# A two-block transformer in fp32 halves: MLP products with hi and lo side by side, and moving weights of 512 columns

## The chip, the cores and the metric

The kernel runs on one core of a Trainium2 chip. The metric is the device time of one execution in microseconds. The kernel before took 950.4 us (median of three runs, 950.13 to 951.17).

## The reference, cut to what matters

The input is one sequence of 256 tokens with 1024 features. It passes two blocks of two layers each: in the first block MoBA with forgetting attention, then differential with sliding-window attention; in the second block MLA, a cross-attention to a memory of 256 tokens and an MLP, then a stick-breaking attention, again a cross-attention and an MLP. The change touches the cross-attention's memory side and the MLP:

```python
def mem_cross_attn(h, m, w_q, w_kv, w_o):
    q = (h @ w_q).reshape(B, S, MEM_HEADS, MEM_HEAD_DIM)
    kv = (m @ w_kv).reshape(B, m.shape[1], 2, MEM_HEADS, MEM_HEAD_DIM)   # 1024 -> 512 keys, 512 values
    ...
def sq_relu_mlp(h, w_in, w_out):                                          # 1024 -> 4096 -> 1024
    return jnp.square(jax.nn.relu(h @ w_in)) @ w_out
```

All arrays are float32.

## The kernel before, in words

Each projection is made of three matmuls in fp32r. A weight and an activation are each split into a rounded part (hi) and the rest (lo); the product is hi x hi + hi x lo + lo x hi, summed in PSUM. Weights come from HBM by SyncE's queue in pieces of 512 KB ([128, 1024]); `wpiece` and `split` (lines 635 to 656) cut each in two parts of 512 columns, copy the hi part (ScalarE or VectorE) and subtract for the lo part (VectorE). Activations are kept by features (`x` as four tiles [128, 2, 256]), and `new_T` (line 715) makes the split tiles: for chunks of 128 features hi and lo tiles that each hold two chunks.

There are two kinds of projection. `mm_feat` has 128 weight columns stationary and 256 tokens moving, so the result stands by features. `mm_tok` has 128 tokens stationary and up to 512 weight columns moving, so the result stands by tokens.

`mlp` (line 1533) runs G = 8 groups of 512 hidden features. `hidden(g)` makes a group: `proj_feat` with four blocks of 128 features, two to a PSUM bank of 512 columns; per block ReLU out of PSUM, a square, and a split. Its product with `wout` goes on into four accumulator banks that live through the whole MLP; the group after is started before it. The first MLP (`final=False`) does this product with `mm_feat` and adds each bank to `x` by `add_x`, times a broadcast scale (`rstd_bc`). The second (`final=True`) does it with `mm_tok`.

`mem_kv(l)` makes a memory's keys and values for one cross-attention. It is written ahead of the stage that needs it and depends on nothing in it, so its parts fill gaps. The values are made in two passes of 256 columns, both token tiles side by side in one bank; each half is drained when its pass is done.

The order of the work is not written by hand: `Plan.schedule` (line 303) simulates the engines with a table of costs and starts, on each engine, the ready operation with the longest way to the end. It reckons N/2.4 + 2 ns for an fp32r matmul of N columns, a transfer at 360 bytes per ns plus `LANDING`, and it adds to each priority a random number of spread `SHAKE` (0 before). A buffer of a pool (8 PSUM banks; classes acc, S, T, O, F have upper limits) is given ahead of its turn only while enough stay for what comes before it in the program. All instructions are issued from one helper, so nearly every record carries line 569; matmuls are told apart by shape. Tiles carry their pool's name: `k` is float32, `r` is fp32r, `psum` a bank.

Of the kernel before, what the change touches and what calls it, by code (L numbers as in the profile page):

```python
# [14 lines left out]
AF = mybir.ActivationFunctionType  # L15
OP = mybir.AluOpType
# [137 lines left out]

AHEAD = 4000.0

LANDING = 2500.0

FIRST = {"T": 1200.0, "A": 700.0, "V": 1200.0, "G": 800.0, "S": 730.0}

SHAKE, SEED = 0.0, 0

LAT = {("T", "A"): 196, ("T", "V"): 196, ("T", "G"): 196, ("A", "T"): 271, ("V", "T"): 256, ("G", "T"): 203,
       ("A", "A"): 143, ("V", "V"): 127, ("G", "G"): 102, ("A", "V"): 142, ("V", "A"): 128, ("A", "G"): 170,
# [9 lines left out]
class Plan:  # L174
# [95 lines left out]
    def schedule(self):  # L270
# [58 lines left out]
        while n < len(ops):  # L329
# [72 lines left out]
            if o.kind == "dma_start":  # L402
# [3 lines left out]
                free[e] = t + issue  # L406
                o.start, o.end = t, st + d + LANDING
            else:
# [165 lines left out]
S = 256  # L574
D = 1024
NT = 2
NC8 = D // 128
FF = 4096
# [52 lines left out]
class Net:  # L631
# [82 lines left out]

    def new_T(self, n=NC8):

        res = []
        for nm in ("xh", "xl"):
            v = []
            for c0 in range(0, n, 2):  # L720
                t = self.r2([128, min(2, n - c0), 256], nm)
                v += [t[:, c] for c in range(min(2, n - c0))]
            res.append(v)
        return res

    def mm3(self, ps, st, mv, first, last):

# [731 lines left out]
    def mem_kv(self, l):  # L1459

        w = self.a["xa_w_kv_2"][l]
        mt = self.gained(self.memT, 48 + 8 * l)
        kT = self.new_T(4)
        for b in range(4):
            ps = self.ps("F")[:, :256]
            for wh, wl, k, n in self.wtiles(w, 0, NC8, b * 128, 128, "f"):
                for i in range(n):
                    self.mm_feat(ps, k + i == 0, mt, wh[:, i], wl[:, i], k + i, k + i == NC8 - 1)
            y = self.t2([128, 256], "xy")
            self.nc.vector.tensor_tensor(y, ps, self.rmem_bc, op=OP.mult)  # L1470
            self.split(y, kT[0][b], kT[1][b])
        v = [[self.r2([128, 512], "xv") for _ in range(NT)] for _ in range(2)]
        for b in range(2):
            ps = self.ps("F")
            for wh, wl, k, n in self.wtiles(w, 0, NC8, 512 + b * 256, 256, "f"):
                for t in range(NT):
                    s = slice(t * 128, (t + 1) * 128)
                    for i in range(n):
                        h, lo = mt[0][k + i][:, s], mt[1][k + i][:, s]
                        o = ps[:, t * 256:(t + 1) * 256]  # L1480
                        f = dict(stop=False, skip_group_check=True)
                        self.nc.tensor.matmul(o, h, wh[:, i], start=k + i == 0 and t == 0, **f)
                        self.nc.tensor.matmul(o, h, wl[:, i], start=False, **f)
                        f["stop"] = k + i == NC8 - 1
                        self.nc.tensor.matmul(o, lo, wh[:, i], start=False, **f)
            for t in range(NT):
                o = slice(b * 256, (b + 1) * 256)
                self.evac_split(v[0][t][:, o], v[1][t][:, o], ps[:, t * 256:(t + 1) * 256], self.rmem[:, t:t + 1])
        self.xk[l], self.xv[l] = kT, v

    def cross(self, l):
# [41 lines left out]
    def mlp(self, l, final=False):  # L1533
        nc, a, xt = self.nc, self.a, self.xt
        win, wout = a["mlp_w_in_2"][l], a["mlp_w_out_2"][l]
        G = FF // 512
        if final:
            nc.boost = 2e4
            xf = self.x_tok()
            nc.seen = nc.ops[-1]  # L1540
            nc.boost = 0.0
        else:
            rb2 = self.rstd_bc(self.rstd2)
        acc = [self.acc() for _ in range(4)]

        def hidden(g):
            ps = self.proj_feat(win, xt, g * 512, 512, cls=("S", "T") if g % 2 else ("S", "O"))
            h = self.new_T(4)
            for b, p in enumerate(ps):
                for i in range(2):  # L1550
                    sq = self.t2([128, 256], "msq")
                    pi = p[:, i * 256:(i + 1) * 256]
                    r = self.t2([128, 256], "mr")
                    nc.scalar.activation(r, pi, AF.Relu)
                    nc.either(("V", "tensor_tensor", (sq, r, r), {"op": OP.mult}),
                              ("A", "activation", (sq, r, AF.Square), {}))
                    self.evac_split(h[0][2 * b + i], h[1][2 * b + i], sq)
            return h

        h = hidden(0)  # L1560
        for g in range(G):
            hn = hidden(g + 1) if g + 1 < G else None
            if final:
                pieces = [(hf, p) for hf in range(2) for p in self.wtiles(wout, 4 * g, 4, hf * 512, 512)]
                pieces = [(t, *p) for p in pieces for t in range(NT)]
                if g == G - 1:

                    rest = self.ps("S")
                    end = [(wh[:, :, c:c + 256], wl[:, :, c:c + 256], k, n, c) for c in (0, 256)
                           for t, hf, (wh, wl, k, n) in pieces if (t, hf) == (1, 1)]  # L1570
                    pieces = [p for p in pieces if p[:2] != (1, 1)]
                for t, hf, (wh, wl, k, n) in pieces:
                    nc.boost = 0.0 if g < G - 1 else 6e3 - 1.5e3 * (2 * hf + t)
                    self.mm_tok(acc[2 * hf + t], h, wh, wl, n, k - 4 * g, t, k == 0, k + n == FF // 128)
                nc.boost = 0.0
                if g == G - 1:
                    for wh, wl, k, n, c in end:
                        nc.boost = 1.0e3 if c == 0 else 0.0
                        self.mm_tok((rest if c else acc[3])[:, 0:256], h, wh, wl, n, k - 4 * g, 1, c > 0 and k == 4 * g,
                                    k + n == FF // 128)  # L1580
                    nc.boost = 0.0
                h = hn
                continue
            for hf in range(2):
                for wh, wl, k, n in self.wtiles(wout, 4 * g, 4, hf * 512, 512):
                    for b in range(4):
                        bank = 2 * hf + b // 2
                        o = acc[bank][:, (b % 2) * 256:(b % 2) * 256 + 256]
                        s = slice(b * 128, (b + 1) * 128)
                        for j in range(n):  # L1590
                            self.mm_feat(o, k + j == 0 and b % 2 == 0, h, wh[:, j, s], wl[:, j, s], k + j - 4 * g,
                                         k + j == 4 * G - 1)
                        if k + n == 4 * G and b % 2:
                            self.add_x(acc[bank], bank, rb2)
            h = hn
        if final:
            self.finish(xf, acc, rest)
# [187 lines left out]
```

## Time and profile before

| | |
|---|---|
| runs, median (lowest to highest) | 950.4 us (950.13 to 951.17) |
| the profiled execution, its own time | 950.25 us |
| its span, first to last instruction | 948.5 us |
| mean granted TensorE clock | 0.999 of full |
| HBM read | 154.89 MB |

Times below are microseconds from the start of the span unless marked ns. A stretch is a window of the span. "Busy" is the time in which an engine had at least one instruction running; matmul records overlap, since the engine is pipelined, so the mean ns of a matmul's record is longer than the distance to the next one.

### The profile page before, as it was taken

How to read it: one execution, taken by the hardware profiler on the slowest of the kernel's cores; microseconds unless marked ns; L12 is line 12 of the kernel's file. 1: busy time of each engine (PE TensorE's matmuls, PEld its weight loads, DVE VectorE, ACT ScalarE, POOL GpSimd, SP SyncE). 2: the span in 40 equal slices, each digit the busy share in tenths (PEclk: the TensorE clock that was granted, in tenths of full speed). 3: DMA queues.
4: the chain of work that ended last, by engine and by line, in shares of the span. 5: the costliest groups of instructions: out<-in, count | busy, mean ns of one | idle time of the engine just before them, and what ended most of it. 6: DMA issues, size and time to landing. Idle time of an engine off the chain costs nothing.

```text
span 948.5 us, 18213 instructions
## 1 busy us (share of the span) xinstructions
PE 934.5 (99%) x6852; PEld 874.0 (92%) x6852; DVE 675.1 (71%) x1568; ACT 579.7 (61%) x1317; POOL 57.1 (6%) x96
## 2 busy tenths in 40 slices
PE   8999999999999999999999999999999999999997
PEld 7898898889899999999999999999899999999986
DVE  9799978778978658974555556846859876666564
ACT  7687965687576856755554556536856745333353
POOL 1160000311401000000000000000000000000000
PEclk9999999999999999999999999999999999999999
DMA  8755346445325526554554667445526455555641
GB/s 312 233 177 178 111 142 219 158 128 157 122 79 167 167 68 202 176 156 124 171 193 160 221 217 233 134 151 179 178 67 203 135 174 178 182 193 192 199 147 44
DMA packets 45512, 157.12 MB, mean 166 GB/s; under 512 B 5352, under 2 KB 5488, under 8 KB 45424
## 3 DMA queue, kind: packets, MB, share of 16 engines
q1 hardware_dynamic: 44784, 154.59, 50.6%
q8 instruction: 53, 0.87, 0.4%
q0 software_dynamic: 352, 1.06, 0.3%
q10 hardware_dynamic: 288, 0.32, 0.1%
q14 instruction: 35, 0.29, 0.1%
HBM read 154.89 MB, written 1.06 MB: 164 GB/s over the span
## 4 chain that ended last, share of the span: by engine, by line
PE 92%; DVE 4%; DMA 1%; ACT 1%; issue 1%; POOL 0%; POOLq 0%; ACTq 0%; DVEq 0%; SPq 0%
PE psum L569 92%; DVE k L569 2%; DVE r L569 2%; DMA k<-in_w_in_ab_dram 1%; ACT r L569 1%; DMA k<-in_consts_dram 1%; ACT k L569 0%; POOL k L569 0%; POOLq L1779 0%; ACTq L569 0%; DVEq L569 0%; SPq L569 0%; POOLq L569 0%
## 5 line engine op out<-in xcount | busy, mean ns | idle before, releaser
L569 PE MATMUL psum<-r,r 128*128 128x256 f32 (+1 forms) x6078 | 884.3, 303 | 3.0 <-ACT r L569 2.0
L569 PEld LDWEIGHTS psum<-r,r 128*128 128x128 f32 x6078 | 802.9, 190 | 49.1 <-issue 5.7
L569 DVE TENSOR_TENSOR r<-k,r 128x512 fp32r<-128x512 f32 (+4 forms) x681 | 413.3, 644 | 159.9 <-PE psum L569 109.3
L569 ACT ACTIVATE r<-k 128x512 fp32r<-128x512 f32 (+2 forms) x587 | 321.1, 591 | 182.0 <-PE psum L569 150.4
L569 ACT ACTIVATE k<-psum 128x256 f32<-128x256 f32 (+4 forms) x163 | 68.0, 446 | 122.0 <-PE psum L569 119.7
L569 PE MATMUL psum<-k,k 128*128 128x128 f32 (+7 forms) x746 | 130.8, 304 | 3.0 <-DVE k L569 2.3
L569 PEld LDWEIGHTS psum<-k,k 128*128 128x128 f32 (+2 forms) x746 | 89.5, 166 | 16.4 <-DVE k L569 5.0
L569 POOL TENSOR_TENSOR k<-k,k 128x2 f32<-128x2 f32 (+3 forms) x42 | 48.1, 1162 | 860.7 <-DVE k L569 808.4
L569 ACT ACTIVATE k<-k 128x256 f32<-128x256 f32 (+5 forms) x154 | 73.0, 501 | 14.0 <-DVE k L569 10.7
L569 ACT ACTIVATE k<-k,k 128x256 f32<-128x256 f32 (+3 forms) x139 | 59.5, 447 | 8.8 <-DVE k L569 6.7
L569 DVE CAST r<-k 128x512 fp32r<-128x512 f32 (+3 forms) x94 | 36.4, 393 | 15.3 <-PE psum L569 7.4
L569 DVE TENSOR_TENSOR k<-k,k 128x512 f32<-128x512 f32 (+5 forms) x93 | 44.7, 491 | 1.6 <-ACT k L569 1.1
L569 DVE TENSOR_TENSOR k<-psum,k 128x512 f32<-128x512 f32 (+2 forms) x61 | 36.7, 607 | 11.6 <-PE psum L569 11.0
L569 ACT ACTIVATE r<-k,k 128x256 fp32r<-128x256 f32 x76 | 35.0, 500 | 12.1 <-DVE k L569 11.2
L569 DVE SCALAR_TENSOR_TENSOR r<-k,k,r 128x256 fp32r<-128x256 f32 x80 | 36.4, 478 | 0.7 <-PE psum L569 0.6
L569 DVE TENSOR_TENSOR k<-k 128x256 f32<-128x256 f32 (+3 forms) x34 | 11.8, 346 | 27.3 <-ACT k L569 25.8
L569 DVE TENSOR_TENSOR r<-psum,r 128x256 fp32r<-128x256 f32 (+1 forms) x36 | 18.0, 508 | 15.5 <-ACT r L569 14.3
L569 ACT ACTIVATE r<-psum 128x256 fp32r<-128x256 f32 (+1 forms) x36 | 16.2, 455 | 19.7 <-PE psum L569 19.6
L569 DVE TENSOR_SCALAR k<-k,k 128x8 f32<-128x8 f32 (+6 forms) x100 | 25.1, 282 | 1.5 <-POOL k L569 0.9
L569 DVE SCALAR_TENSOR_TENSOR k<-psum,k 128x256 f32<-128x256 f32 (+2 forms) x24 | 12.2, 508 | 5.6 <-PE psum L569 4.9
L469 ACT ACT_TABLE_LOAD x12 | 15.4, 1283 | 0.2
L569 DVE CUSTOM_DVE_ANT_0 k<-psum,k 128x256 f32<-128x256 f32 (+1 forms) x48 | 15.0, 350 | 0.6 <-PE psum L569 0.6
(39 smaller groups left out, 160.2 us busy)
## 6 DMA issues: line engine op xcount, KB each, us to landing
k<-in_mlp_w_in_dram SPq DMA_DIRECT2D x64, 512.0 KB, 4.3
k<-in_mlp_w_out_dram SPq DMA_DIRECT2D x64, 512.0 KB, 4.2
k<-in_w_in_ab_dram SPq DMA_DIRECT2D x29, 512.0 KB, 5.4
k<-in_w_in_cd_dram SPq DMA_DIRECT2D x26, 512.0 KB, 4.1
k<-in_sb_w_qkv_dram SPq DMA_DIRECT2D x24, 512.0 KB, 4.2
k<-in_xa_w_kv_dram SPq DMA_DIRECT2D x16, 512.0 KB, 4.2
k<-in_w_out_ab_dram SPq DMA_DIRECT2D x8, 512.0 KB, 3.9
k<-in_w_out_cd_dram SPq DMA_DIRECT2D x8, 512.0 KB, 3.8
```

The costliest lines, as they stand in the source:

```text
L469: self.nc.scalar.preload_act_table_set(table)
L569: return getattr(eng, method)(*[real(a) for a in args], **{k: real(v) for k, v in kw.items()})
```

## The change

- `new_T` makes one tile [128, 512] for each chunk, hi in columns 0 to 255, lo in 256 to 511, in place of separate hi and lo tiles of two chunks.
- `hidden(g)` goes over a group in two pairs of blocks. Each block has a PSUM bank of its own. Per chunk, wh meets the whole tile (512 columns: hi and lo) and wl meets the hi half (256 columns, into the first half of the bank). The two halves are then added: a copy of the second half, an add, and one instruction for max(r, 0) x r. The weight pieces are 4 chunks x 256 columns, before 2 chunks x 512.
- The first MLP's second product uses `mm_tok`; at its end each of the four accumulators is scaled by tokens, turned by 16 transposes and added to `x`. The broadcast scale is dropped there.
- `mem_kv` makes the values by `proj_tok` with 512 columns, in two banks of class F at once.
- The planner's `LANDING` goes from 2500 to 3500 ns, `SHAKE` from 0 to 150 ns with seed 9.

```diff
-LANDING = 2500.0
+LANDING = 3500.0
...
-SHAKE, SEED = 0.0, 0
+SHAKE, SEED = 150.0, 9
...
     def new_T(self, n=NC8):
-        res = []
-        for nm in ("xh", "xl"):
-            v = []
-            for c0 in range(0, n, 2):
-                t = self.r2([128, min(2, n - c0), 256], nm)
-                v += [t[:, c] for c in range(min(2, n - c0))]
-            res.append(v)
-        return res
+        t = [self.r2([128, 512], "xt") for _ in range(n)]
+        return [u[:, 0:256] for u in t], [u[:, 256:512] for u in t], t
...
         v = [[self.r2([128, 512], "xv") for _ in range(NT)] for _ in range(2)]
-        for b in range(2):
-            ps = self.ps("F")
-            for wh, wl, k, n in self.wtiles(w, 0, NC8, 512 + b * 256, 256, "f"):
-                for t in range(NT):
-                    s = slice(t * 128, (t + 1) * 128)
-                    for i in range(n):
-                        h, lo = mt[0][k + i][:, s], mt[1][k + i][:, s]
-                        o = ps[:, t * 256:(t + 1) * 256]
-                        f = dict(stop=False, skip_group_check=True)
-                        self.nc.tensor.matmul(o, h, wh[:, i], start=k + i == 0 and t == 0, **f)
-                        self.nc.tensor.matmul(o, h, wl[:, i], start=False, **f)
-                        f["stop"] = k + i == NC8 - 1
-                        self.nc.tensor.matmul(o, lo, wh[:, i], start=False, **f)
-            for t in range(NT):
-                o = slice(b * 256, (b + 1) * 256)
-                self.evac_split(v[0][t][:, o], v[1][t][:, o], ps[:, t * 256:(t + 1) * 256], self.rmem[:, t:t + 1])
+        for t, ps in enumerate(self.proj_tok(w, mt, 512, 512, cls="F", fill="f")):
+            self.evac_split(v[0][t], v[1][t], ps, self.rmem[:, t:t + 1])
...
-        else:
-            rb2 = self.rstd_bc(self.rstd2)
...
         def hidden(g):
-            ps = self.proj_feat(win, xt, g * 512, 512, cls=("S", "T") if g % 2 else ("S", "O"))
             h = self.new_T(4)
-            for b, p in enumerate(ps):
-                for i in range(2):
+            for b2 in range(2):
+                ps = [self.ps("S", "hid"), self.ps("T" if b2 else "O", "hid")]
+                for wh, wl, k, n in self.wtiles(win, 0, NC8, g * 512 + b2 * 256, 256):
+                    for b, p in enumerate(ps):
+                        s = slice(b * 128, (b + 1) * 128)
+                        for i in range(n):
+                            f = dict(skip_group_check=True)
+                            nc.tensor.matmul(p, wh[:, i, s], xt[2][k + i], start=k + i == 0, stop=False, **f)
+                            nc.tensor.matmul(p[:, 0:256], wl[:, i, s], xt[0][k + i], start=False,
+                                             stop=k + i == NC8 - 1, **f)
+                for b, p in enumerate(ps):
+                    r = self.t2([128, 256], "mr")
+                    half = self.t2([128, 256], "mh")
+                    nc.scalar.activation(half, p[:, 256:512], AF.Copy)
+                    nc.vector.tensor_tensor(r, p[:, 0:256], half, op=OP.add)
                     sq = self.t2([128, 256], "msq")
-                    pi = p[:, i * 256:(i + 1) * 256]
-                    r = self.t2([128, 256], "mr")
-                    nc.scalar.activation(r, pi, AF.Relu)
-                    nc.either(("V", "tensor_tensor", (sq, r, r), {"op": OP.mult}),
-                              ("A", "activation", (sq, r, AF.Square), {}))
-                    self.evac_split(h[0][2 * b + i], h[1][2 * b + i], sq)
+                    nc.vector.scalar_tensor_tensor(sq, r, 0.0, r, op0=OP.max, op1=OP.mult)
+                    self.evac_split(h[0][2 * b2 + b], h[1][2 * b2 + b], sq)
             return h
...
                 for wh, wl, k, n in self.wtiles(wout, 4 * g, 4, hf * 512, 512):
-                    for b in range(4):
-                        bank = 2 * hf + b // 2
-                        o = acc[bank][:, (b % 2) * 256:(b % 2) * 256 + 256]
-                        s = slice(b * 128, (b + 1) * 128)
-                        for j in range(n):
-                            self.mm_feat(o, k + j == 0 and b % 2 == 0, h, wh[:, j, s], wl[:, j, s], k + j - 4 * g,
-                                         k + j == 4 * G - 1)
-                        if k + n == 4 * G and b % 2:
-                            self.add_x(acc[bank], bank, rb2)
+                    for t in range(NT):
+                        self.mm_tok(acc[2 * hf + t], h, wh, wl, n, k - 4 * g, t, k == 0, k + n == FF // 128)
+                if g == G - 1:
+                    y = []
+                    for t in range(NT):
+                        y.append(self.t2([128, 512], "my"))
+                        self.scaled(y[t], acc[2 * hf + t], self.rstd2[:, t:t + 1])
+                    for b in range(2):
+                        p = self.ps("T")
+                        for c in range(2):
+                            for t in range(NT):
+                                o = (2 * b + c) * 128
+                                self.tr(p[:, (2 * c + t) * 128:(2 * c + t + 1) * 128], y[t][:, o:o + 128])
+                        self.add_x(p, 2 * hf + b)
```

## Rows read from the trace of the kernel before

**Rows 1.** The page: busy us, share and instructions of each engine; granted clock in 40 slices.
```profile
PE 934.5 (99%) x6852; PEld 874.0 (92%) x6852; DVE 675.1 (71%) x1568; ACT 579.7 (61%) x1317; POOL 57.1 (6%) x96
...
PEclk9999999999999999999999999999999999999999
```
**Rows 2.** The page: the chain that ended last, share of the span by engine.
```profile
PE 92%; DVE 4%; DMA 1%; ACT 1%; issue 1%; POOL 0%; POOLq 0%; ACTq 0%; DVEq 0%; SPq 0%
```
**Rows 3.** Groups by form, TensorE: tiles, shapes, count | busy us, mean ns | idle before.
```profile
L569 PE MATMUL psum<-r,r 128*128 128x256 f32 x5064 | 704.7, 286 | 1.5 <-DVE r L569 0.7 <-ACT r L569 0.7
L569 PE MATMUL psum<-r,r 128*128 128x512 f32 x918 | 264.3, 396 | 1.5 <-ACT r L569 1.3 <-DVE r L569 0.2
```
**Rows 4.** Timeline of TensorE, 455.8 to 475: start, us of the whole row, form, count.
```profile
455.78 19.42 PE L569 MATMUL psum<-r,r 128*128 128x256 f32 x160
```
**Rows 5.** Timeline of TensorE, 929 to 937.
```profile
928.80 8.55 PE L569 MATMUL psum<-r,r 128*128 128x512 f32 x37
```
**Rows 6.** Timeline of TensorE, 800 to 900: both forms, named by the first.
```profile
799.75 100.50 PE L569 MATMUL psum<-r,r 128*128 128x256 f32 x643
```
**Rows 7.** Groups by form, TensorE, of the same stretch, 800 to 900.
```profile
L569 PE MATMUL psum<-r,r 128*128 128x256 f32 x428 | 77.2, 280 | 0.0
L569 PE MATMUL psum<-r,r 128*128 128x512 f32 x215 | 74.5, 394 | 0.0
```
**Rows 8.** Table by stretch, 430 to 575: length, busy us and count of each engine, clock, DMA.
```profile
430.00:575.00 145.00, 145.00 (x1215) 145.00 (x1215) 80.55 (x148) 76.58 (x165) 0.70 (x1) 1.00 0.59 188
```
**Rows 9.** Groups by form over the whole span, VectorE and ScalarE.
```profile
L569 DVE TENSOR_TENSOR r<-k,r 128x512 fp32r<-128x512 f32 x561 | 367.5, 688 | 119.1 <-PE psum L569 87.1 <-ACT r L569 17.0 <-issue 12.7
L569 ACT ACTIVATE r<-k 128x512 fp32r<-128x512 f32 x490 | 286.1, 624 | 164.0 <-PE psum L569 145.7 <-DMA k<-in_w_in_ab_dram 5.4 <-DVE r L569 3.7
...
L569 DVE TENSOR_TENSOR r<-k,r 128x256 fp32r<-128x256 f32 x96 | 39.2, 426 | 36.5 <-PE psum L569 20.8 <-ACT r L569 15.3
...
L569 DVE SCALAR_TENSOR_TENSOR r<-k,k,r 128x256 fp32r<-128x256 f32 x80 | 36.4, 478 | 0.7 <-PE psum L569 0.6
L569 ACT ACTIVATE r<-k,k 128x256 fp32r<-128x256 f32 x76 | 35.0, 500 | 12.1 <-DVE k L569 11.2 <-PE psum L569 0.7
...
L569 DVE CAST r<-k 128x512 fp32r<-128x512 f32 x71 | 29.8, 424 | 6.1 <-PE psum L569 5.4 <-DMA k<-in_w_in_ab_dram 0.7
...
L569 ACT ACTIVATE k<-psum 128x256 f32<-128x256 f32 x75 | 25.4, 378 | 96.7 <-PE psum L569 95.8 <-DVE r L569 0.9
...
L569 DVE TENSOR_TENSOR k<-psum,k 128x256 f32<-128x256 f32 x16 | 6.7, 420 | 3.8 <-PE psum L569 3.4 <-ACT k L569 0.2
...
L569 DVE SCALAR_TENSOR_TENSOR k<-k,k,k 128x256 f32<-128x256 f32 x12 | 5.6, 476 | 0.3 <-ACT k L569 0.3
...
L569 DVE SCALAR_TENSOR_TENSOR k<-psum,k,k 128x512 f32<-128x512 f32 x4 | 3.0, 751 | 5.3 <-PE psum L569 5.3
```
**Rows 10.** Timeline at the end of both cross-attentions, TensorE: in brackets idle before and releaser.
```profile
397.36 0.39 PE L569 MATMUL psum<-r,r 128*128 128x256 f32 x1 [0.73 <-DVE r L569]
...
745.18 0.39 PE L569 MATMUL psum<-r,r 128*128 128x256 f32 x1 [0.39 <-ACT r L569]
```
**Rows 11.** Timeline of TensorE from 393.66: transposes (128 columns, k,k) among fp32r products.
```profile
393.66 0.27 PE L569 MATMUL psum<-k,k 128*128 128x128 f32 x1
393.69 0.37 PE L569 MATMUL psum<-r,r 128*128 128x256 f32 x1
393.90 0.27 PE L569 MATMUL psum<-k,k 128*128 128x128 f32 x1
393.92 0.37 PE L569 MATMUL psum<-r,r 128*128 128x256 f32 x1
```
**Rows 12.** Timeline at the end of the first MLP, 596 to 616: VectorE's adds and TensorE.
```profile
595.60 1.29 DVE L569 TENSOR_TENSOR k<-psum,k 128x512 f32<-128x512 f32 x2 [1.27 <-PE psum L569]
595.76 12.63 PE L569 MATMUL psum<-r,r 128*128 128x256 f32 x104
```
**Rows 13.** The page: DMA issues, count, KB each, median us from issue to landing.
```profile
k<-in_mlp_w_in_dram SPq DMA_DIRECT2D x64, 512.0 KB, 4.3
```

## The prediction

> **What bounds the kernel now.** I read the page's engine shares first, then its chain, then the groups by form, then stretches of TensorE's own timeline. TensorE is busy 99% of the 948.5 us span and the granted clock is at its upper level (2.4 GHz) in all forty slices [rows 1]; the chain that ended last runs 92% through matmuls into PSUM [rows 2]. Busy share alone proves little, because matmul records overlap: a 128x256 product has a record of 286 ns but takes up far less of the engine. What decides is the distance from one matmul to the next, and the groups say which forms there are: 5064 of 256 moving columns, 918 of 512, and before both together 3.0 us of idle [rows 3].
>
> The distance is read from stretches with nothing but one form. From 455.78 us, 160 products of 256 columns take 19.42 us: less the last record's 0.28, over 159 steps, 120.4 ns each [rows 4]. From 928.80 us, 37 products of 512 take 8.55 us: (8.55 - 0.39)/36 = 226.7 ns each [rows 5]. So 256 more columns cost 106.3 ns, and 14.1 ns of each matmul do not depend on its columns. This is the number on which the forecast stands. The test is a mixed stretch: from 799.75 to 900.25 us the second MLP runs 643 products [rows 6], 428 of 256 and 215 of 512 [rows 7]; 427 x 120.4 + 215 x 226.7 = 100.15 us, against 100.50 - 0.39 = 100.11 us measured. The two prices hold when the forms alternate, and these 100 us hold no wait at all. In the first MLP (430 to 575 us) TensorE and its weight loads are both busy throughout, VectorE 56%, ScalarE 53% [rows 8]. The kernel there goes as fast as matmuls can be issued; only fewer or narrower matmuls help.
>
> **Part 1, first products of both MLPs.** Now each of 8 groups x 4 blocks x 8 chunks needs three products of 256 (wh with x's hi, wh with x's lo, wl with x's hi). After, hi and lo lie side by side, and wh meets both in one product of 512; wl's stays. The columns are the same, the matmuls two in place of three: 256 removed a layer, 512 in all, each worth 14.1 ns [rows 4, 5]: 7.2 us off the bounding engine.
>
> What it adds: a block's halves must be summed. Before: ReLU out of PSUM, a square, the split. After: copy of the lo half (ScalarE, 378 ns), an add that reads PSUM (VectorE, 420), a combined max-and-multiply (476), the split (its lo 426) [rows 9]. VectorE's load for one MLP group is then 16 weight splits x 688 + 4 x (420 + 476 + 426) = 16.3 us, against 32 x (226.7 + 120.4) + 48 x 226.7 = 22.0 us of TensorE: 74%. I cost it at nothing; TensorE's own products hide it. That cover would be gone if VectorE also took all hi copies of the weights (16 x 424 ns [rows 9] make 23.1 us, 1.1 a group and 9 an MLP too many), but those are ScalarE's first, whose 16 x 624 + 4 x 378 = 11.5 us leave room.
>
> PSUM: a pair of blocks now fills two banks in 5.6 us where four blocks filled two in 11.6. With four accumulators there are two pairs, so one is drained (2 x 1.3 us of VectorE by the rows above) while the other fills: nothing, as long as memory's products don't hold banks (first rival).
>
> The entry into each MLP changes. The first pass over all eight chunks now takes 5.6 us, not 11.6, while chunks are still being made at 500 ns (ScalarE) and 478 (VectorE) each [rows 9]. The second pair's products on early chunks can cover it. Nothing in the trace shows this order. Below it costs nothing (a gain is out: the only waits of TensorE near the entries are those priced in Part 3), above 2 us an entry (four late chunks at 500 ns); I take 0.5 each, the size of the waits seen there [rows 10]: 1.0 us.
>
> **Part 2, second product of the first MLP.** 768 products of 256 become 384 of 512, now with the hidden values as weights: 384 x 14.1 = 5.4 us. The result then stands by tokens and must be turned: four scalings and 16 transposes. Where transposes and 256-column products alternate, a pair takes 0.23 to 0.24 us [rows 11], so a transpose costs 0.11: 1.8 us. The broadcast of the scale, two products of that size, goes: 0.2. Net 1.6 us added; half of it, 0.8, if a row of four is cheaper than single ones, and 2.5 if each four also waits once for its bank (about 0.2). The longer way from the last accumulator to the next layer (scaling, transposes, add in place of multiply, add) lengthens a chain by about a microsecond; today 104 products run on without a break while that chain's DVE part is done [rows 12], and they remain: nothing. Without them it would be 1 us.
>
> **Part 3, memory's values.** 96 products of 256 a layer become 48 of 512: 96 x 14.1 = 1.4 us in both layers. But the two halves of the columns were finished apart; heads 0 and 1 could go ahead. Now all four heads wait for both token tiles, each drained at 512 columns (751 ns for a lo [rows 9]). At both cross-attentions TensorE already waits for exactly this drain: 0.73 us for a VectorE split near 397 us, 0.39 us for ScalarE near 745 [rows 10]. Bounds: -1.1 us in all if the new order starts the values earlier, +3 if each waits for two full drains more (2 x 751). I take 0.6 each, nearest the waits shown: 1.2 us.
>
> **The rest.** Transfers keep their number and size. The planner's landing constant goes from 2.5 to 3.5 us, nearer to the 4.3 us that MLP weights take [rows 13]; TensorE shows almost no wait for data, so this brings nothing. Planner constants and random priorities reorder every stage: between -1.5 and +2 us, as all of TensorE's idle is 3.0 us [rows 3]; I take zero.
>
> **The sum.** The profiled execution took 950.25 us, 948.5 of it span; the three runs have a median of 950.4. 950.25 - 7.2 - 5.4 - 1.4 + 1.6 + 1.0 + 1.2 = 940.1; forecast 940.0.
>
> **Rivals.** *First: memory's values take the banks.* They hold two PSUM banks from their first to their last product, as low-priority fill during the attention or MLP ahead; before, one. With four accumulators and one pair of hidden banks, no second pair is left, so each pair's drain (two chains of about 378 + 420 ns and the hand-overs) may stand open. 16 pairs of the first MLP x 0.3 us, or as much in the attention stages that also lose a bank: about 5 us, 945. For: two of eight banks are a lot. Against: the second product is ready work all that time, and in the trace's MLPs nothing waits [rows 6, 8].
> *Second, the other side: time goes by columns.* The columns of the first products don't change (3 x 256 = 512 + 256), nor those of the others. If the 14.1 ns belong not to each matmul but to something that stays (a 512-column product then takes up to 2 x 120.4 = 240.8 ns), nothing is saved and the 3.8 us of additions remain: 954.1, slower. It decides from the saving per removed matmul: under 3.8 us/992 = 3.8 ns the change loses; between 2 and 5.7 ns it lies within the bound of no change, about 950.4. Against it: 226.7 in place of 240.8 ns [rows 4, 5], and the mixed stretch adds up by the same prices [rows 6, 7]. The Trainium skill (TensorE: Matmul & The Clock Gate, section Back-to-back issue gap) has a rule of this kind: an isolated gap of N/2.4 + 2.5 ns at full clock, by which, as an estimate, the 992 matmuls removed would give back 2.5 us in all and the kernel would take 951.6 us. The trace differs from it, with 226.7 and 120.4 ns where the rule says 215.8 and 109.2.
> *Third: the new order is better by itself.* The waits at both cross-attentions and the entries go, and additions are hidden: 950.25 - 14.0 + 0.8 - 1.1 = 936.0.
>
> **How the numbers follow.** Forecast, 937 to 943: 66%. First rival, 943 to 948.5: 20%, and 3% more beyond that. Second rival: 3% with nothing saved, 3% with little saved and the time within the bound of no change. Third, under 937: 4%. A remainder of 1% for slower by lost cover. A measurement of this kernel can tell about 0.2%, 948.5 to 952.3, from no change; so faster 0.90, same 0.06, slower 0.04. The range 936.5 to 946.0 holds the forecast and the larger part of the first rival.
>
> **What would show it.** In the profile after: 992 fewer fp32r matmuls, 16 transposes more; in the MLPs 512-column products at about 227 ns and 256-column ones at about 120, with VectorE near 70% there. If the pairs 512 + 256 take over 355 ns, Part 1's price is wrong. A wait of TensorE for VectorE at the cross-attentions of over 1.5 us would show Part 3's addition too small; idle inside an MLP, the first rival. The prediction is wrong altogether if the stretch of the first MLP shrinks by less than 8 us.

## The result, and the profile after

The changed kernel takes 945.0 us (median of four runs, 944.15 to 946.09) against 950.6: a ratio of 0.9945, 95% interval 0.9933 to 0.9958. It is faster, inside the range given (936.5 to 946.0), but by 5.4 us in the profiled execution (950.25 to 944.87) where 10.3 were forecast. The later runs show that two errors met, one in a price, one in the order of the work, and that some of the additions did not come.

The page after: engine shares, and the chain by engine.

```profile
PE 929.3 (99%) x5872; PEld 825.1 (87%) x5872; DVE 706.8 (75%) x1625; ACT 579.6 (61%) x1305; POOL 58.4 (6%) x96
...
PE 95%; DVE 2%; ACT 1%; issue 1%; DMA 0%; POOLq 0%; POOL 0%; ACTq 0%; DVEq 0%
```

980 fewer matmul records stand there than in [rows 1] (992 removed, 16 transposes added, 2 dropped make 978; the other 2 can be records missing from either trace), and TensorE is still busy 99% of a span that is 0.6% shorter: 14% fewer matmuls bought little. The chain has even more of TensorE in it than in [rows 2]. VectorE rose from 71 to 75%, as the added halves demand.

Next, what all waits of TensorE in the changed kernel add up to, by releaser: us in total, times, longest.

```profile
PE psum L569 <- DVE k L569: 2.6, 3, 1.4
PE psum L569 <- ACT k L569: 1.9, 3, 0.7
PE psum L569 <- POOL k L569: 1.2, 1, 1.2
PE psum L569 <- ACT r L569: 0.8, 1, 0.8
PE psum L569 <- DVE r L569: 0.4, 2, 0.2
```

Together 6.9 us; the same view of the kernel before sums to 7.0. So the missing 5 us are not in the sum of the waits that this view lists. They lie in what a matmul takes, or in stalls that the view does not list. Two stretches of TensorE's timeline, one in each MLP, with their groups by form (the second pair of rows belongs to the second stretch):

```profile
477.76 97.58 PE L569 MATMUL psum<-r,r 128*128 128x512 f32 x490
...
L569 PE MATMUL psum<-r,r 128*128 128x512 f32 x348 | 96.2, 394 | 0.0
L569 PE MATMUL psum<-r,r 128*128 128x256 f32 x142 | 36.8, 280 | 0.0
...
819.68 100.56 PE L569 MATMUL psum<-r,r 128*128 128x512 f32 x504
...
L569 PE MATMUL psum<-r,r 128*128 128x512 f32 x363 | 98.7, 393 | 0.0
L569 PE MATMUL psum<-r,r 128*128 128x256 f32 x141 | 35.6, 279 | 0.0
```

At the forecast's prices, 226.7 and 120.4 ns [rows 4, 5], the second takes 362 x 226.7 + 141 x 120.4 = 99.04 us; it took 100.56 - 0.39 = 100.17. The first: 347 x 226.7 + 142 x 120.4 = 95.76 against 97.19. That is 3.1 and 4.1 ns more for each 512-column product, without a wait in sight. Over 640 of them an MLP this would be 4.6 us of the gain: 14.0 - 4.6 = 9.4. That is an estimate from two stretches, and so is 944.7 us, the sum with the forecast's 3.8 us of additions: it meets the measured 944.87, but by accident: the runs below show that the additions were smaller and that the order cost something too. Yet in the mixed stretch of before [rows 6, 7] the same prices had come out within 0.06 us.

### The profile page after: what moved, and what is told of

It reads as the page before. It is cut to its first block, busy times and chain, and to the rows that moved or that the text cites. A ratio compares the mean times of both kernels' runs of the same rounds, so it can differ in the third digit from the quotient of the medians.

```text
span 943.1 us, 16261 instructions
## 1 busy us (share of the span) xinstructions
PE 929.3 (99%) x5872; PEld 825.1 (87%) x5872; DVE 706.8 (75%) x1625; ACT 579.6 (61%) x1305; POOL 58.4 (6%) x96
## 4 chain that ended last, share of the span: by engine, by line
PE 95%; DVE 2%; ACT 1%; issue 1%; DMA 0%; POOLq 0%; POOL 0%; ACTq 0%; DVEq 0%
PE psum L569 95%; DVE k L569 1%; DVE r L569 1%; ACT k L569 1%; ACT r L569 1%; DMA k<-in_consts_dram 0%; POOLq L1773 0%; POOL k L569 0%; ACTq L569 0%; DVEq L569 0%; POOLq L569 0%
## 5 line engine op out<-in xcount | busy, mean ns | idle before, releaser
L569 PE MATMUL psum<-r,r 128*128 128x256 f32 (+1 forms) x5086 | 866.9, 328 | 1.6 <-ACT r L569 0.8
L569 PEld LDWEIGHTS psum<-r,r 128*128 128x128 f32 x5086 | 746.2, 189 | 88.3 <-issue 4.2
L569 DVE TENSOR_TENSOR r<-k,r 128x512 fp32r<-128x512 f32 (+2 forms) x681 | 416.1, 644 | 105.6 <-PE psum L569 66.6
L569 ACT ACTIVATE r<-k 128x512 fp32r<-128x512 f32 (+3 forms) x624 | 340.5, 588 | 162.4 <-PE psum L569 107.8
L569 PE MATMUL psum<-k,k 128*128 128x128 f32 (+6 forms) x758 | 124.4, 308 | 4.5 <-DVE k L569 2.6
L569 DVE TENSOR_TENSOR k<-psum,k 128x256 f32<-128x256 f32 (+1 forms) x125 | 63.8, 513 | 67.2 <-ACT k L569 46.9
L569 ACT ACTIVATE k<-k 128x512 f32<-128x512 f32 (+5 forms) x104 | 54.3, 541 | 17.5 <-DVE k L569 15.0
L569 DVE SCALAR_TENSOR_TENSOR k<-k 128x256 f32<-128x256 f32 (+2 forms) x67 | 27.6, 412 | 1.9 <-DMA k<-in_consts_dram 0.6
L569 DVE CAST r<-k 128x512 fp32r<-128x512 f32 (+2 forms) x57 | 22.3, 398 | 8.8 <-PE psum L569 8.1
L569 ACT ACTIVATE k<-psum,k 128x512 f32<-128x512 f32 (+2 forms) x24 | 14.6, 621 | 9.2 <-PE psum L569 9.1
```

What stands on the lines that cost most here:

```text
L569: return getattr(eng, method)(*[real(a) for a in args], **{k: real(v) for k, v in kw.items()})
```

## The experiments

Four theories were put against one another. A: the price of the record holds, and the shortfall comes from elsewhere. B: the price of a 512-column product was too low for a stream that holds 256-column products as well. C: memory's values in two banks take the gain away. D: the planner's order, which every edit upsets, decides over more than the record allowed.

**Each part alone.** The three runs take one part's lines of the diff each, into the kernel before, with its planner's constants. For the first: `new_T` and `hidden` as in the diff; for the second, with the scalings and transposes of the diff behind it:

```diff
-        else:
-            rb2 = self.rstd_bc(self.rstd2)
...
+                    for t in range(NT):
+                        self.mm_tok(acc[2 * hf + t], h, wh, wl, n, k - 4 * g, t, k == 0, k + n == FF // 128)
```

and for the third only the values of `mem_kv`:

```diff
+        for t, ps in enumerate(self.proj_tok(w, mt, 512, 512, cls="F", fill="f")):
+            self.evac_split(v[0][t], v[1][t], ps, self.rmem[:, t:t + 1])
```

> The kernel before with the first products of both MLPs alone changed (hi and lo side by side). Theory A, the 14.1 ns price of the record holds and the shortfall comes from elsewhere: 7.2 us gained, 1.0 lost at the entries, ratio 0.9935. Theory B, the price was mis-sized: a 512-column product among other forms takes about 231.6 ns and a 256-column one about 117 (stretch 800 to 900 of the changed kernel: 361 x 231.6 + 144 x 117 = 100.4 us). Then the second MLP gains 768 x 117.3 + 384 x 232 - 640 x 231.6 - 256 x 117 = 1.0 us and the first 1536 x 120 - 256 x 231.6 - 1024 x 117 = 5.2: 6.2 us less 0 to 1, ratio 0.9935 to 0.9945, and the stretch of the second MLP shows it: at most 1.5 us shorter under B, 3.6 under A.

Measured: 959.6 us, ratio 1.0097 (1.0081 to 1.0112). Both expectations fell: 9 us slower, not 6 faster.

> The kernel before with the first MLP's second product alone changed. Theory A: 5.4 us gained, 1.6 lost to the transposes, ratio 0.9960. Theory B: 768 x 117.3 + 384 x 232 = 179.2 us in place of 184.3, 5.1 gained less 1.6: ratio 0.9963. The two differ in the sum: under A parts 1 and 2 add up (12.6 us of TensorE), under B they don't, for together they leave 640 x 231.6 + 256 x 117 = 178.2 us an MLP, 7.1 less than before in both.

Measured: 960.2 us, ratio 1.0100 (1.0086 to 1.0114). The same again.

> The kernel before with memory's values alone in one pass of 512 columns. By the record 1.4 us gained and 1.2 lost at the cross-attentions: ratio 0.9998. Theory C, that memory's values in two banks take away the gain of the other parts: 2 to 5 us slower alone, ratio 1.002 to 1.005, with more waits of TensorE.

Measured: 952.6 us, ratio 1.0026 (1.0016 to 1.0035). In the size of theory C, with three waits (0.60, 0.56 and 0.55 us at 324 to 329 us, inside MLA) that the kernel before has not. The second bank alone does not make them: the changed kernel has that bank too and not these waits. In another order of the changed kernel (parts_old_order, below) three such waits come back. How much of the 2 us is the bank's and how much the order's stays open.

This run also tests the price. Its second MLP has the same products as the kernel before, 2 of 256 columns for one of 512, only in another order:

```profile
799.73 100.57 PE L569 MATMUL psum<-r,r 128*128 128x256 f32 x641
...
L569 PE MATMUL psum<-r,r 128*128 128x256 f32 x427 | 77.3, 281 | 0.0
L569 PE MATMUL psum<-r,r 128*128 128x512 f32 x214 | 74.5, 396 | 0.0
```

The forecast's prices give 213 x 226.7 + 427 x 120.4 = 99.70 us; it took 100.57 - 0.39 = 100.18. That is 2.2 ns more for each product of 512, with no wait and at a granted clock of 1.00. The stretch of before, whose last product is also one of 512, gives 214 x 226.7 + 428 x 120.4 = 100.05 against 100.11: 0.3 ns. In the runs of the second part alone, of `new_T` alone and of the two constants alone (both below), whose second MLPs have these products too, the stretch from 819.8 us shows 2.3, 2.9 and 1.6 ns. So the agreement on which the forecast relied belongs to one order of these products and not to their proportion.

Where the first part alone loses is far from the part. The timeline of TensorE there at 322 to 350 us, in the middle of MLA, rows with a wait:

```profile
331.04 0.38 PE L569 MATMUL psum<-r,r 128*128 128x256 f32 x1 [1.28 <-ACT r L569]
332.17 2.99 PE L569 MATMUL psum<-r,r 128*128 128x256 f32 x23 [0.75 <-DVE r L569]
336.45 0.38 PE L569 MATMUL psum<-r,r 128*128 128x256 f32 x1 [1.29 <-ACT r L569]
337.62 6.75 PE L569 MATMUL psum<-r,r 128*128 128x256 f32 x27 [0.79 <-DVE r L569]
345.04 5.17 PE L569 MATMUL psum<-r,r 128*128 128x256 f32 x41 [0.67 <-DVE r L569]
```

In the kernel before no wait of TensorE stands between 322 and 350 us. The run of the second part alone has such a row at 640 to 651 us, in the stick-breaking attention (0.31 to 2.29 us). The MLP itself did gain with the first part: from the last wait at the second cross-attention to the end of the span are 957.8 - 756.85 = 200.95 us here, 943.1 - 742.11 = 200.99 in the changed kernel, and 948.5 - 745.18 = 203.3 before. 2.3 us less, where the record's price would have 3.6, or 3.1 with 0.5 for the entry. That lies between theory B's 1.5 at most and theory A's 3.6. So over the whole second MLP 0.8 to 1.3 us are missing; the stretch above, at 640 x 3.1 ns, made it 2.0. The 4.6 us for both MLPs may be too high by as much.

**The order by itself.** Two kernels in which no matmul differs from the kernel before. In the first only the tiles of `new_T`:

```diff
+        t = [self.r2([128, 512], "xt") for _ in range(n)]
+        return [u[:, 0:256] for u in t], [u[:, 256:512] for u in t], t
```

> The kernel before with new_T alone changed (one split tile for each chunk): not one matmul differs, only the buffers and with them the planner's order. Theory D, that the 10 us lost by each part alone are the order's (a row of waits of TensorE at 329 to 344 us in the run with part 1 alone, 8 us): the same row of waits stands here, and without part 1's 6 us of gain the kernel is 10 to 16 us slower, ratio 1.011 to 1.017. The record's view of the order (between -1.5 and +2 us): ratio 0.9985 to 1.002, and then part 1 itself has cost its 9 us.

Measured: 965.9 us, ratio 1.0162 (1.0149 to 1.0176): 16 us for a change of buffers. The same row of waits is there. Timeline at 330 to 338 us, VectorE and TensorE:

```profile
330.83 0.43 DVE L569 CAST r<-k 128x512 fp32r<-128x512 f32 x1 [2.05 <-DMA k<-in_xa_w_kv_dram]
...
331.57 0.38 PE L569 MATMUL psum<-r,r 128*128 128x256 f32 x1 [1.32 <-ACT r L569]
332.71 3.00 PE L569 MATMUL psum<-r,r 128*128 128x256 f32 x23 [0.76 <-DVE r L569]
...
337.39 0.39 PE L569 MATMUL psum<-r,r 128*128 128x256 f32 x1 [1.68 <-ACT r L569]
```

TensorE waits for the split of a weight, and the split for a piece of memory's weights (`in_xa_w_kv`) to land. In these rows TensorE has nothing else to run while it waits, though memory's products were meant as fill. The table by stretch, 325 to 350 us, and a part of it, of this run, then of the kernel before (length, busy us and count of PE, PEld, DVE, ACT, POOL, granted clock, DMA):

```profile
325.00:350.00 25.00, 20.10 (x134) 18.57 (x133) 10.63 (x21) 7.79 (x15) 0.00 (x0) 0.86 0.35 106
...
337.80:344.50 6.70, 6.25 (x26) 5.73 (x27) 1.70 (x3) 1.32 (x3) 0.00 (x0) 0.50 0.31 86
```

```profile
325.00:350.00 25.00, 25.00 (x189) 23.97 (x189) 14.08 (x45) 17.45 (x48) 0.00 (x0) 1.00 0.25 85
```

134 matmuls in place of 189, and a mean granted clock of 0.86: after the waits of 1.32, 0.76 and 1.68 us TensorE ran from 337.8 to 344.5 us at 0.50, the lower of its two levels (1.2 GHz).

The second kernel changes two constants:

```diff
-LANDING = 2500.0
+LANDING = 3500.0
...
-SHAKE, SEED = 0.0, 0
+SHAKE, SEED = 150.0, 9
```

> The kernel before with the planner's two constants alone changed (landing 3500, random priorities of spread 150 with seed 9). Theory D: the order is worth far more than the record's -1.5 to +2 us; 5 to 20 us slower here, ratio 1.005 to 1.02, with new waits in the attention stages. The record: ratio 0.9985 to 1.002.

Measured: 969.8 us, ratio 1.0201 (1.0188 to 1.0214). An order can cost 19.6 us here; of the three that were run, the kernel before had the best. The planner's own reckoning points the same way: `Plan.schedule`, run for these kernels, leaves TensorE 7.9 us without work in the kernel before, 23.9 with `new_T` alone and 29.1 with the two constants, so 16.0 and 21.2 more, where the chip took 15.8 and 19.6 us longer. For the three parts alone it leaves 25.0, 18.0 and 11.8 us.

**Other orders of the changed kernel.** All do the work of the diff.

> All three parts with the planner's constants as in the kernel before (landing 2500, no random priorities; 15.1 us without work in the plan, 14.0 in the changed kernel). Theory D: 944 to 948, that is, the constants are worth about 1 us here, though alone in the kernel before they cost 19. If the constants were the gain of the changed kernel: over 950.

```diff
-LANDING = 3500.0
+LANDING = 2500.0
...
-SHAKE, SEED = 150.0, 9
+SHAKE, SEED = 0.0, 0
```

Measured: 949.3 us, ratio 0.9987 (0.9977 to 0.9996). 4.3 us over the changed kernel, 1.3 past the expectation, though the planner sees only 1.1 us more without work: with three parts the same two constants gain 4 us, with none of them they cost 19.

> The changed kernel with a planner that reckons N/2.4 + 13.5 ns for an fp32r matmul, landing 2500 and another seed (7, spread 200): same work, another order. Theory D: fewer waits outside the MLPs, 2 to 6 us less than the changed kernel, 939 to 943; the prices in the MLPs stay (231 and 117 ns), so it doesn't reach the 937.7 that the record's price gives without any new wait. If the order were worth at most 2 us: 943 to 947.

```diff
-LANDING = 3500.0
+LANDING = 2500.0
...
-SHAKE, SEED = 150.0, 9
+SHAKE, SEED = 200.0, 7
...
-            cost = N * (1 if N >= 256 else 4) / 2.4 + 2
+            cost = N * (1 if N >= 256 else 4) / 2.4 + 13.5
```

Measured: 949.6 us, ratio 0.9994 (0.9984 to 1.0003). A miss for theory D: the planner leaves TensorE 7.4 us without work in this order, less than in any other, and it is 4.6 us slower. A truer price did not make a truer plan. TensorE's waits sum to 9.9 us here, 3.0 more than in the changed kernel, and from 250.3 to 253.6 us the granted clock is 0.50, as in the changed kernel (below). The rest was not followed further.

The next two keep the planner's price and change constants alone, `LANDING` to 2500.0 in both:

> The changed kernel, its planner as it was priced before (landing 2500), with seed 42 and spread 300: of some 380 seeds the order in which the planner leaves TensorE least without work (8.4 us, 14.0 in the changed kernel, 7.9 in the kernel before). Theory D: what the planner leaves idle comes back on the chip; 4 to 7 us less than the changed kernel, 938 to 941. If the chip's waits have little to do with the planner's: 943 to 949, as with the order from the corrected price.

```diff
-SHAKE, SEED = 150.0, 9
+SHAKE, SEED = 300.0, 42
```

Measured: 940.7 us, ratio 0.9898 (0.9883 to 0.9913).

> The same with seed 52 and spread 50, which leaves TensorE 9.5 us without work in the plan. Theory D: 939 to 942, within 2 us of the other. The rival: 943 to 949.

```diff
-SHAKE, SEED = 150.0, 9
+SHAKE, SEED = 50.0, 52
```

Measured: 941.1 us, ratio 0.9904 (0.9889 to 0.9919). Both as theory D has it: at the same prices, the two orders with the least idle in the plan are the two fastest, though 1.1 us of idle between parts_old_order and the changed kernel went with 4.3 us on the chip. TensorE's waits in the first of the two:

```profile
PE psum L569 <- DVE k L569: 1.4, 2, 1.0
PE psum L569 <- POOL k L569: 1.2, 1, 1.2
PE psum L569 <- ACT r L569: 1.1, 1, 1.1
PE psum L569 <- DVE r L569: 0.4, 2, 0.2
PE psum L569 <- ACT k L569: 0.2, 1, 0.2
```

4.3 us, 2.6 less than in the changed kernel. Most of the rest of the 4 us between them shows in the clock. The table by stretch where the first block ends and MLA begins, for the kernel before, the changed kernel (with a part of it) and this order:

```profile
245.00:263.00 18.00, 16.40 (x131) 13.34 (x131) 17.14 (x64) 12.41 (x45) 6.15 (x7) 1.00 0.32 94
```

```profile
245.00:263.00 18.00, 14.76 (x103) 11.12 (x102) 16.45 (x73) 15.00 (x56) 3.16 (x4) 0.91 0.19 56
257.30:260.60 3.30, 3.30 (x16) 2.26 (x17) 2.75 (x10) 2.47 (x11) 0.00 (x0) 0.50 0.51 149
```

```profile
245.00:263.00 18.00, 16.88 (x133) 14.80 (x135) 16.15 (x62) 13.79 (x48) 5.18 (x6) 1.00 0.46 147
```

In the changed kernel TensorE waits 0.84, 0.35, 1.37 and 0.69 us between 249 and 257 us, and then runs 3.3 us at the lower level of its clock; in the kernel before and in this order the granted clock stays at 1.00. At half the clock 3.3 us lose some 1.6 us, an estimate, and 2.6 + 1.6 is about the 4 us. These two orders beat both kernels.

**The price by itself.** Two kernels of nothing but streams of matmuls. `a1` is a product of 256 columns, `b1` and `b2` are of 512, `b2` with the roles of weights and activations changed; `run` issues a list of them. The first:

```diff
+    run([a1] * 180)
+    run([b1] * 90)
+    run([b2] * 90)
+    run([b1, a1] * 60)
+    run([b1, a1, b2, b1, a1, b2, b2] * 16)
+    run(([b1] * 16 + [a1] * 16 + [b2] * 24) * 2)
+    run([b1, b2] * 45)
```

> Streams of fp32r matmuls by themselves, one after the other, everything else of the network left out: 180 of 256 columns; 90 of 512 with weights stationary; 90 of 512 with tokens stationary; 60 pairs 512 + 256; 16 times the mix of the changed MLP (two of the first, two of 256, three of the second); the same mix in runs of 16, 16 and 24; the two kinds of 512 in turn. No other engine works. Theory A: 120.4 and 226.7 ns in all streams, a pair 347 ns. Theory B with its cause in the mix of forms: 120 and 227 in the pure ones, 231 to 233 for the 512 and 117 for the 256 in pairs and mix, a pair 349 to 351. Theory B with its cause in the other engines' traffic: 347 a pair here, more only where other engines work.

Timeline of TensorE: 180 of 256, 90 of 512 with weights stationary, 60 pairs, the mix of the changed MLP, the same mix in long runs, the two kinds of 512 in turn (a stream is named by its first form).

```profile
12.48 23.33 PE L568 MATMUL psum<-r,r 128*128 128x256 f32 x180
...
35.79 20.68 PE L568 MATMUL psum<-r,r 128*128 128x512 f32 x90
...
77.12 21.43 PE L568 MATMUL psum<-r,r 128*128 128x512 f32 x120
...
98.53 22.60 PE L568 MATMUL psum<-r,r 128*128 128x512 f32 x112
...
121.11 22.30 PE L568 MATMUL psum<-r,r 128*128 128x512 f32 x112
...
143.39 20.70 PE L568 MATMUL psum<-r,r 128*128 128x512 f32 x90
```

Read one by one, the starts in the two pure streams lie 120 and 227 ns apart, but for the first of each; in the stream of 256 the first fifteen or so lie 213 apart, which is why its row is long. In the pairs they lie 236.6 ns apart after one of 512 and 116.5 after one of 256: 353.1 a pair, not 347.1, and also past theory B's 349 to 351. Two pairs of three take 349 to 350 ns, and the third, the first one in the other bank, 361. The mix, 80 of 512 and 32 of 256, takes 0.30 us more than the same products in long runs: 3.8 ns for each of 512, the size found in the MLPs. The two kinds of 512 in turn take what one kind takes, so a change of roles without a change of width costs nothing. No other engine works in these streams. So theory B holds without the other engines: a mix of widths costs what neither width costs alone with the same banks and weights. What in the mix costs it, these streams do not separate.

The second has pairs in runs of 1 to 48, two of 256 to one of 512, and then some of it again while VectorE, ScalarE and the transfers work:

```diff
+    for k in (1, 2, 4, 12, 48):
+        run(([b1] * k + [a1] * k) * (48 // k))
+    run([b2, a1, a1] * 32)
...
+    run([b1, a1] * 48)
+    run([b2, a1, a1] * 32)
```

> Streams of fp32r matmuls by themselves, the rest of the network left out: 96 of 256 columns, 48 of 512, then the same 48 and 48 of both in runs of 1, 2, 4, 12 and 48; 32 times one of 512 and two of 256 (the second MLP before). After that VectorE, ScalarE and the transfers work without pause beside 16 of 512 with tokens stationary, 96 of 256, 48 of 512, 48 pairs and again the 32. Theory B with its cause in the change of width: 48 x (226.7 + 120.4) = 16.66 us in runs of 48, rising to about 17.0 in single pairs (354.5 ns a pair in the streams before); the loaded half takes the same times. With the other engines' traffic as a second cause, the loaded streams take 1 to 3% more. In the stream with two of 256 to one of 512 little is added, 32 x 467.5 = 14.96 us, as in the second MLP before.

```profile
36.26 17.20 PE L568 MATMUL psum<-r,r 128*128 128x512 f32 x96
...
53.43 16.97 PE L568 MATMUL psum<-r,r 128*128 128x512 f32 x96
...
70.37 17.06 PE L568 MATMUL psum<-r,r 128*128 128x512 f32 x96
...
87.41 16.97 PE L568 MATMUL psum<-r,r 128*128 128x512 f32 x96
...
104.37 16.91 PE L568 MATMUL psum<-r,r 128*128 128x512 f32 x96
...
121.26 15.21 PE L568 MATMUL psum<-r,r 128*128 128x512 f32 x96
...
140.32 11.75 PE L568 MATMUL psum<-r,r 128*128 128x256 f32 x96
...
152.05 11.16 PE L568 MATMUL psum<-r,r 128*128 128x512 f32 x48
...
163.19 17.19 PE L568 MATMUL psum<-r,r 128*128 128x512 f32 x96
...
180.36 15.21 PE L568 MATMUL psum<-r,r 128*128 128x512 f32 x96
```

The first five rows are the same 96 products as pairs and in runs of 2, 4, 12 and 48: 17.20, 16.97, 17.06, 16.97 and 16.91 us. The cost does not simply fall with the length of the runs: runs of two give back four fifths of it, runs of four only half. The pairs under load (the row at 163.19) take what they took in quiet, and so do the 32 times one of 512 and two of 256 (121.26 and 180.36). That the load was there, the table by stretch shows: in the pairs under load VectorE and ScalarE are busy throughout and the transfers run at 240 GB/s; in the quiet stretch nothing else works. In the last stream the transfers go on, but VectorE and ScalarE run out of work on the way.

```profile
41.00:53.00 12.00, 12.00 (x70) 10.41 (x70) 0.00 (x0) 0.00 (x0) 0.00 (x0) 1.00 0.01 1
...
164.00:180.00 16.00, 16.00 (x93) 13.89 (x92) 16.00 (x28) 16.00 (x32) 0.00 (x0) 1.00 0.77 240
```

And the proportion that misled the record: in one product of 512 and two of 256, the starts lie 231.5, 117.2 and 118.9 ns apart, together 467.6, where 226.7 + 2 x 120.4 = 467.5. In this stream the mix costs nothing; in the pairs it costs 6 ns a pair. But the two streams differ in more than the proportion: the pairs use `b1`, with weights stationary and in the same banks as `a1`, this one `b2`, with tokens stationary and in banks of its own. And in the run of memory's values alone (above) two of 256 to one of 512 did cost 2.2 ns for each of 512. So the proportion alone does not settle the cost; the order, and perhaps the bank, takes part.

**Runs of one width in the kernel.**

> The changed kernel with the same planner's price, and in which TensorE, among ready matmuls of nearly the same priority (1500 ns), takes one with as many columns as the one before: longer runs of 512 and of 256. Theory B with its cause in the mix of forms: a stretch of 100 us in an MLP holds some 2 to 4% more of its matmuls, 512-column products fall from 231 to about 228 ns, and each MLP is 1 to 2 us shorter: 936 to 942 where waits are as in the other order. Theory B with its cause elsewhere: 231 ns as before and no gain by it.

Beside the price of 13.5 and other constants (`LANDING` 2500.0, `SHAKE, SEED` 100.0, 9):

```diff
-                c, i = next((x for x in near if max(ops[x[1]].other, loader) + ops[x[1]].forms[e][2] <= t + 5), near[0])
+                ok = [x for x in near if max(ops[x[1]].other, loader) + ops[x[1]].forms[e][2] <= t + 5]
+                same = [x for x in ok if ops[x[1]].forms[e][0] == form and x[0] <= ok[0][0] + 1500.0]
+                c, i = (same or ok or near)[0]
+                form = ops[i].forms[e][0]
```

Measured: 951.0 us, ratio 1.0010 (1.0001 to 1.0019). A stretch of the second MLP, and its forms:

```profile
799.71 100.69 PE L572 MATMUL psum<-r,r 128*128 128x512 f32 x506
...
L572 PE MATMUL psum<-r,r 128*128 128x512 f32 x362 | 89.5, 393 | 0.0
L572 PE MATMUL psum<-r,r 128*128 128x256 f32 x144 | 22.9, 281 | 0.0
```

361 x 226.7 + 144 x 120.4 = 99.18 us against 100.30: 3.1 ns for each of 512, as in the changed kernel. The runs there were some ten of 512 and four of 256, and brought nothing; by the streams above, where runs of two and of twelve cost little, length alone does not say why. So this expectation of theory B fell. That a mix of widths can cost is confirmed by the streams; what in it costs, and a way to avoid it inside the kernel, was not found.

## Why the prediction was right or wrong, point by point

- **The bound** (TensorE, by the distance between matmuls): right. The second MLP, where products were only merged, shrank by 2.3 us, and the MLPs hold no waits before or after.
- **The price of 14.1 ns a matmul, Parts 1 to 3**: this step failed, at the sentence "The two prices hold when the forms alternate". The two pure stretches were read nearly rightly (the 160 products of [rows 4] hold one step of 202 ns; the others lie 120 apart, so 13.3 ns would have been truer than 14.1). The test on the mixed stretch was passed by luck of its order: the same products in four other orders take 1.6 to 2.9 ns more for each of 512. In the changed MLPs, with 2.5 of 512 for one of 256, each takes 3.1 to 4.1 ns more. By this estimate the term came to 9.4 us in place of 14.0, or up to 10 by the whole second MLP. What in a mix of widths costs the time stays open.
- **The additions, 3.8 us**: too high. The 16 transposes cost what was reckoned (six in a row at 592.02 us take 0.82, so 0.11 each), and Part 2's 1.6 us stay. The 2.2 us of waits did not come: at the first MLP's entry none stands, at the cross-attentions there were 0.58 us near 396 and 0.59 and 0.21 near 740, against 0.73 and 0.39 [rows 10], and the sum of all waits is 6.9 us against 7.0.
- **Planner constants, "between -1.5 and +2 us; I take zero"**: this step failed too; as a bound it was wrong by ten times. The 3.0 us of [rows 3] are the waits of two groups of products, not "all of TensorE's idle", which is 7.0 us, and idle time bounds what a new order can gain, not what it can lose. Nor was the clock in the sum: the order of the changed kernel let it fall for 3.3 us. Against the best order that was run, the changed kernel's costs about 4 us.
- **The forecast's 940.1, put right by these estimates**: 4.6 us more for the price, 2.2 less for the waits, 1.6 more for the clock make 944.1, where 944.87 was measured. That the total fell inside the range is in part luck, for the errors have opposite signs. For parts_old_order, with 9.9 us of waits and no fall of the clock, the same reckoning falls some 4 us short of the 949.1 measured; what is missing there stays open. In order_42, with about as little idle in the plan as the kernel before, the change is worth 9.7 us, close to the 10.3 forecast: there shorter waits, and the additions that did not come, make up for the price.
- **First rival (banks)**: not in its place, for the MLPs show no waits. The values alone did cost 2 us; by what is open.
- **Second rival (columns)**: a third of it was true: of the 14.1 ns some 9.5 came back for each matmul removed, by the estimate above.
- **Third rival (a better order by itself)**: its mechanism exists, with 940.7 us, and the changed kernel's order is not it.
- **The signs**: "over 355 ns" a pair was set too wide, for in the changed MLPs the two together take about 232 + 117 = 349 ns, under the sign and already over the forecast's 347. "Wrong altogether if the first MLP shrinks by less than 8 us" was not read, because memory's fill moves in and out of this stretch.

The Trainium skill (Perfetto Trace Analysis, section Identifying the Most-Contended Engine) advises to judge how near TensorE is to its limit by the rate of arithmetic reached and by the share of its weight loads, not by the share of its matmuls. In this case neither share told the gain: matmuls stayed at 99%, weight loads fell from 92% to 87% of the span, and the time fell by 0.6%.

## What to carry to other kernels

Read a matmul's price from streams with the mix and the order that the changed kernel will have; a check on one stretch can agree by accident. Where a planner lays out the work, an edit is a new draw of the order as well: measure it in several orders, or a good edit (here two of the parts alone, 9 us slower) looks bad and a lucky constant looks like a gain. And look at the granted clock behind each row of waits: two orders with much the same sum of waits can differ by it.

## What the hardware showed that was not expected

- A 512-column fp32r product in a stream with 256-column ones takes 231 to 237 ns in place of 227, a 256-column one after it about 117 in place of 120. Alternating pairs take 353 ns where the two alone sum to 347; runs of 2, 4 and 12 take less, and not in that order. The same 2 to 1 mix cost 0.3 ns for each of 512 in one order of the kernel and 1.6 to 2.9 in four others. By what mechanism, no run here shows.
- Load on the other engines did not change these times: with VectorE and ScalarE busy throughout and 240 GB/s of transfers, the pairs took 17.19 us against 17.20.
- A row of waits of 0.35 to 1.68 us can come before a fall of the granted clock, and then cost more than its own length: in the changed kernel 0.84, 0.35, 1.37 and 0.69 us between 249 and 257 us, then 3.3 us at 0.50; with `new_T` alone 1.32, 0.76 and 1.68 us, then 6.7 us at 0.50. Not every such row does it: parts_old_order has 1.16, 0.43, 1.49 and 0.62 us between 250 and 263 us, and its clock stays at 1.00.
